# Attention steps of a decoder trunk: divisions on ScalarE, steps at mid-tile, a later begin with convolution taps held back

## The chip, the cores and the metric

The kernel runs on one core of a Trainium2 chip. The metric is the device time of one execution in microseconds. The engines are TensorE (PE, with its weight loads as PEld), VectorE (DVE), ScalarE (ACT), GpSimd (POOL) and SyncE (SP, which issues most transfers). Each engine works through its own queue of instructions in the order in which the program wrote them.

## The reference

One layer of a decoder trunk for a prompt of 2048 tokens and 8 x 4 sample tokens, D_MODEL 1024, in float32. The input projection gives queries (8 heads of 64), keys and values (2 heads), GLU halves for the convolution (512 channels) and two gates of 1024. The part that the change touches, cut down:

```python
def sink_softmax(s, mask, sink):
    s = jnp.where(mask, s, NEG_INF)
    m = jnp.maximum(jnp.max(s, axis=-1, keepdims=True), sink)
    p = jnp.exp(s - m)
    den = jnp.sum(p, axis=-1, keepdims=True) + jnp.exp(sink - m)
    return p / den

def swa_prompt(q, k, v, sinks):          # 16 blocks of 128 queries, each against 256 keys
    ...
    probs = sink_softmax(s, mask, sink)
    o = jnp.einsum('bnkgqs,bnskd->bnqkgd', probs.astype(v.dtype), vb)

def conv_branch(u_hist, conv_w, conv_b, ln_g, ln_b, w_conv_o):
    dw = causal depthwise convolution of width 31 over u = glu_a * sigmoid(glu_b), plus conv_b
    n = LayerNorm(dw)
    return jax.nn.silu(n) @ w_conv_o

# merge: (sigmoid(g_att) * (a @ w_attn_o) + sigmoid(g_conv) * conv) @ w_out, then residual and SwiGLU
```

Queries and keys are rotated on the first 16 of their 64 dims before the scores.

## The kernel before, in words

Everything is kept transposed, channels on the partitions. Tokens are worked on in two groups: group 0 has 1024 columns, in tiles of 512, group 1 has 1056 (the sample tokens last), in tiles of 352. Each float32 product is made of three reduced-precision ones, from operands split into a high and a low half (`hh`, `hl` for activations, `wh`, `wl` for weights). A weight's `wh` is written by ACT (`w_split`, line 242) and its `wl` by POOL (line 243), from raw weights that SP loads. A tile of the input projection is 24 matmuls; `in_order` gives the order of its columns: GLU pairs 0 and 1 (`gb`, `ga`), k, v, the four query tiles `q`, GLU pairs 2 and 3, and 16 gate tiles. `in_evac` empties each result: sigmoid of `gb` on ACT, the GLU product `u<-mm,sg` on DVE, copies of q, k, v and gates (`gst`) on ACT. Between the keys stand small adaLN products (`ada_unit`).

The program is written out in one fixed order by a planner in Python. `Timed` wraps DVE and TensorE: `V.t` and `T.t` add up the planned nanoseconds of what has been issued, by `dve_cost` and `pe_cost`. After each tile `pump` (line 458) lets other work in:

- one step of `tasks` (attention) if `T.t` has reached `task_t`, which then moves on by `task_dt`, 4200 here;
- the weight queue (`w_prefetch`): loads on SP, splits on ACT and POOL;
- one step of each generator in `soon` (the rotations, `rope`, line 953: transfers into `sw`, a product with the sine on POOL, then a product with the cosine and a sum on DVE, one for each pump);
- steps of `bg` for as long as `V.t < T.t + 1400`: mostly the 31 taps for each of four channel tiles of the convolution (`conv_gen`, line 1012; `dw<-u,cw,dw` on DVE, each planned at 1.2 us), then its LayerNorm and SiLU.

`in_done` (line 908) starts the rotation when a query tile is complete; for the fourth it also passes `then`, which appends `attn_gen` (line 1221) to `tasks` after the rotation's last sum and one more pump.

`attn_gen` first splits keys and queries of block 0 (`k_stack`, `q_stack`: high halves `kh`, `qst` on ACT, low halves `kl`, `qst` on POOL); in group 1 a step before it writes the key window out. Each of the group's 8 blocks then has four steps:

1. for the block before, transposes of its second head group and the product with the values (`o`, emptied by ACT as `oa`, `ob`); scores of the first four heads, row maxima on DVE (`p<-ps,mask`, `mx`), exponentials on ACT;
2. `attn_normalise` of these four: `den` and its reciprocal on DVE, four products on POOL (line 1195); the second product with values of the block before; scores of the other four heads;
3. `attn_normalise` of those; `v_block`: a transpose of the values into `pt` and its split into `vz`, high halves on ACT (line 1129), low halves on DVE;
4. transposes of the first four heads' probabilities and their split (`pth` on ACT, `ptl` on DVE); `k_stack` and `q_stack` of the next block.

After the last block `split` turns the four query tiles into `ah` (ACT) and `al` (DVE) for the output projection; group 1 attends the sample tokens before that. `mixer_out` (line 1410) begins by running whatever steps are still in `tasks`, with no tile between them.

PSUM has four buffers `mm` (tiles of the projection, `o`, half of the scores, the adaLN sum), two `ps` and two `pt`. `gemm` can already call `pump` after half of its matmuls (`mid`), which only the last tiles of the merge's output projection use.

Of the kernel before, what the change touches and what calls it, by code (L numbers as in the profile page):

```python
# [12 lines left out]
AF = mybir.ActivationFunctionType  # L13
ALU = mybir.AluOpType
# [115 lines left out]
class Builder:  # L130
# [379 lines left out]
    def gemm_group(self, keys, act, g, evac, hi_first=False, ready=None, chunks=None):  # L510

        units = [self.w_next(k) for k in keys]
        evs = [evac(k) for k in keys]
        chunks = chunks or GROUPS[g]["chunks"]
        for n, (c0, cw) in enumerate(chunks):
            while ready is not None and ready() < c0 + cw:
                self.step(self.bg)
            for u, ev in zip(units, evs):
                ps = self.gemm_tile(u, act, c0, cw, hi_first=hi_first)
                ev(ps, c0, cw)  # L520
                self.pump()
                if n == len(chunks) - 1:
                    self.w_done()
# [384 lines left out]
    def in_done(self, key):  # L908
        nc = self.nc
        kind, g, i = key  # L910
        W = GROUPS[g]["w"]
        if kind == "ga":
            self.u_ready[i] = True
            self.V.tensor_copy(self.uh[:, i], self.u[i][:, 1024:1024 + CW - 1])
            if i == 0:
                self.bg.append(self.conv_gen(g))
        elif kind == "k":
            self.rope(self.kg[:, 128:128 + W], self.sw[0], W)
        elif kind == "q":
            then = (lambda: self.tasks.append(self.attn_gen(g))) if i == 3 else None  # L920
            self.rope(self.q[i][:, :W], self.sw[(i + 1) % 2], W, then)
            if i == 3:
                self.cs = self.sw = None

    def mixer_in(self, g, skip=0):
        order = self.in_order(g)[skip:]
        if g == 1:
            self.boot_state()
            self.tasks += self.finals
            self.task_dt = 4000  # L930
            self.gemm_group(order[:3], self.h, g, self.in_evac, True, lambda: self.h_ready)
            for key in order[:3]:
                self.in_done(key)
            order = order[3:]
        for key in order:
            if key[0] == "k":
                while self.tasks:
                    self.step(self.tasks)
                self.gf = None
                self.task_dt = 4200  # L940
            self.gemm_group([key], self.h, g, self.in_evac)
            self.in_done(key)
            if key == ("gate", g, 14):
                self.gate_start(g)
            self.ada_next()
        self.h = None
# [6 lines left out]
    def rope(self, x, sw, W, then=None):  # L953
        nc = self.nc
        cos, sin = self.cs
        for b in (0, 64):
            nc.scalar.dma_start(out=sw[b:b + 8, :W], in_=x[b + 8:b + 16])
            nc.scalar.dma_start(out=sw[b + 8:b + 16, :W], in_=x[b:b + 8])
        nc.gpsimd.tensor_tensor(out=sw[:80, :W], in0=sw[:80, :W], in1=sin[:80, :W], op=ALU.mult)

        def rest():
            yield None
            self.V.tensor_tensor(out=x[:80], in0=x[:80], in1=cos[:80, :W], op=ALU.mult)
            yield None
            self.V.tensor_tensor(out=x[:80], in0=x[:80], in1=sw[:80, :W], op=ALU.add)
            if then is not None:
                yield None
                then()
        self.soon.append(rest())

# [218 lines left out]
    def attn_normalise(self, st):  # L1189
        nc = self.nc  # L1190
        P, den, es = st
        self.V.tensor_tensor(out=den, in0=den, in1=es, op=ALU.add)
        self.V.reciprocal(out=den, in_=den)
        for j in range(4):
            nc.gpsimd.tensor_scalar(out=P[j], in0=P[j], scalar1=den[:, j:j + 1], scalar2=0.0, op0=ALU.mult, op1=ALU.add)

    def attn_transpose(self, st):
        nc = self.nc
# [973 lines left out]
```

## Time and profile before

| what | value |
|---|---|
| median of 3 runs | 2930.61 us (2924.27 to 2932.72) |
| profiled execution, its own time | 2930.97 us |
| its span | 2927.8 us |
| mean granted TensorE clock | 0.973 |
| busy: PE, PEld, DVE, ACT, POOL | 2738.3, 2573.8, 2039.0, 1187.1, 1672.8 us |

The profile is one execution, with times in us from the start of the span. Input projection and attention of group 0 lie at about 190 to 535 us, those of group 1 at about 1280 to 1718 us. In the rows of a timeline stand start, duration, engine, line, operation, out<-in, shapes and the number of instructions merged, and in brackets the idle time before it on that engine and what ended it. Line 98 is the planner's wrapper, through which all matmuls and most DVE instructions go. In the rows of waits stand who waited for whom, the total, the number of times and the longest. In the rows by stretch PEclk is the TensorE clock that was granted, as a share of full speed.

### The profile page before, as it was taken

How to read it: one execution, taken by the hardware profiler on the slowest of the kernel's cores; microseconds unless marked ns; L12 is line 12 of the kernel's file. 1: busy time of each engine (PE TensorE's matmuls, PEld its weight loads, DVE VectorE, ACT ScalarE, POOL GpSimd, SP SyncE). 2: the span in 40 equal slices, each digit the busy share in tenths (PEclk: the TensorE clock that was granted, in tenths of full speed). 3: DMA queues.
4: the chain of work that ended last, by engine and by line, in shares of the span. 5: the costliest groups of instructions: out<-in, count | busy, mean ns of one | idle time of the engine just before them, and what ended most of it. 6: DMA issues, size and time to landing. Idle time of an engine off the chain costs nothing. (4 is left out here: it accounts for less than half of the span.)

```text
span 2927.8 us, 43739 instructions
## 1 busy us (share of the span) xinstructions
PE 2738.3 (94%) x16046; PEld 2573.8 (88%) x16046; DVE 2039.0 (70%) x3304; ACT 1187.1 (41%) x2410; POOL 1672.8 (57%) x1305
## 2 busy tenths in 40 slices
PE   8997899999899999998788999989999998999998
PEld 4775677789899999898778999979999997999997
DVE  5999963365766666779997436587766665677676
ACT  4334466433433333431555443343343334333333
POOL 1367776334666666455675222476677667666664
PEclk9998999999999999999899999999999998999999
DMA  7542232443222222431111333433333355222221
GB/s 279 151 115 69 76 104 91 139 141 124 89 76 75 85 80 73 127 103 44 40 57 60 102 120 125 152 122 100 112 114 105 102 187 167 66 76 76 80 72 63
DMA packets 364601, 302.94 MB, mean 103 GB/s; under 512 B 33483, under 2 KB 321111, under 8 KB 364365
## 3 DMA queue, kind: packets, MB, share of 16 engines
q1 hardware_dynamic: 347621, 276.02, 30.8%
q10 hardware_dynamic: 16768, 24.15, 2.6%
q8 instruction: 127, 2.08, 0.3%
q14 instruction: 85, 0.70, 0.1%
HBM read 249.98 MB, written 50.23 MB: 103 GB/s over the span
## 5 line engine op out<-in xcount | busy, mean ns | idle before, releaser
L243 POOL TENSOR_TENSOR wl<-wr,wh 128x512 fp32r<-128x512 f32 (+1 forms) x470 | 893.5, 1915 | 634.5 <-ACT wh L242 571.1
L98 PE MATMUL mm<-third,wh 128*128 128x352 f32 (+1 forms) x2323 | 568.4, 325 | 6.6 <-DVE u L98 3.7
L242 ACT ACTIVATE wh<-wr 128x512 fp32r<-128x512 f32 (+1 forms) x470 | 372.4, 810 | 282.2 <-PE mm L98 125.9
L98 PE MATMUL mm<-hh,wh 128*128 128x352 f32 (+1 forms) x1200 | 436.0, 363 | 30.5 <-DVE u L98 11.2
L98 PE MATMUL mm<-hh,wl 128*128 128x352 f32 (+1 forms) x1200 | 426.4, 355 | 0.0
L98 PEld LDWEIGHTS mm<-third,wh 128*128 128x128 f32 x2323 | 407.7, 190 | 12.1 <-DVE third L98 6.6
L98 PE MATMUL mm<-hl,wh 128*128 128x352 f32 (+1 forms) x1200 | 416.6, 356 | 1.3 <-DVE hl L98 1.3
L243 POOL TENSOR_TENSOR wl<-s,wh 128x512 fp32r<-128x512 f32 x198 | 259.1, 1317 | 261.8 <-ACT wh L242 249.7
L98 DVE SCALAR_TENSOR_TENSOR dw<-u,cw,dw 128x1024 f32<-128x1024 f32 x240 | 393.4, 1652 | 4.7
L98 PE MATMUL mm<-third,wl 128*128 128x352 f32 (+1 forms) x1187 | 383.2, 323 | 0.6 <-POOL wl L243 0.6
L98 PE MATMUL mm<-mh,wh 128*128 128x352 f32 (+1 forms) x1048 | 340.1, 325 | 3.4 <-DVE third L98 1.8
L98 PE MATMUL mm<-ml,wh 128*128 128x352 f32 (+1 forms) x1048 | 334.8, 324 | 4.2 <-ACT wh L242 2.5
L98 PE MATMUL pt<-third,wh 128*128 128x352 f32 (+1 forms) x1189 | 292.2, 325 | 10.9 <-ACT y L1982 5.3
L98 DVE SCALAR_TENSOR_TENSOR third<-mm,mod_G,third 128x352 f32<-128x352 f32 (+2 forms) x408 | 223.7, 565 | 95.5 <-PE mm L98 78.3
L98 PEld LDWEIGHTS mm<-hh,wh 128*128 128x128 f32 x1200 | 230.1, 192 | 63.2 <-DVE u L98 12.1
L242 ACT ACTIVATE wh<-s 128x512 fp32r<-128x512 f32 x198 | 120.9, 626 | 383.7 <-PE mm L98 190.7
L98 PE MATMUL mm<-mh,wl 128*128 128x336 f32 (+1 forms) x824 | 266.1, 323 | 5.7 <-POOL wl L243 5.7
L98 PEld LDWEIGHTS mm<-hl,wh 128*128 128x128 f32 x1200 | 228.8, 192 | 22.9 <-DVE hl L98 1.9
L98 PEld LDWEIGHTS mm<-hh,wl 128*128 128x128 f32 x1200 | 229.3, 191 | 21.5
L98 PEld LDWEIGHTS mm<-third,wl 128*128 128x128 f32 x1187 | 225.3, 190 | 0.9 <-POOL wl L243 0.9
L98 PEld LDWEIGHTS pt<-third,wh 128*128 128x128 f32 x1189 | 209.8, 191 | 12.7 <-ACT y L1982 5.8
L98 PEld LDWEIGHTS mm<-mh,wh 128*128 128x128 f32 x1048 | 200.3, 191 | 4.6 <-DVE third L98 2.1
(357 smaller groups left out, 5504.5 us busy)
## 6 DMA issues: line engine op xcount, KB each, us to landing
wr<-in_w_ffn_in SPq DMA_DIRECT2D x132, 512.0 KB
wr<-in_w_ffn_out SPq DMA_DIRECT2D x66, 512.0 KB
wr<-in_w_in SPq DMA_DIRECT2D x52, 512.0 KB
wr<-in_w_ada SPq DMA_DIRECT2D x48, 512.0 KB
wr<-in_w_out SPq DMA_DIRECT2D x32, 512.0 KB
gl<-gate SPq DMA_DIRECT2D x64, 176.0 KB
third<-op_p SPq DMA_DIRECT2D x56, 176.0 KB
gate<-gst ACTq DMA_DIRECT2D x48, 176.0 KB
```

What stands on the lines that cost most here:

```text
L98: return f(*args, **kw)
L242: self.nc.scalar.activation(out=hi, in_=src, func=AF.Copy)
L243: self.nc.gpsimd.tensor_tensor(out=lo, in0=src, in1=hi.bitcast(F32), op=ALU.subtract)
```

## The change

Four edits. The mid-tile `pump` is switched on in `gemm_group` for tiles of 512 columns while `tasks` is not empty, and `task_dt` is 6000 instead of 4200 in group 0. When the fourth query tile is done, the planner's DVE clock is put 10 us ahead, so that `pump` issues no `bg` work until TensorE's planned time has caught up; this holds in both groups. The rotation of the fourth query tile is followed by two pumps instead of one before `attn_gen` is appended. In `attn_normalise` the four products with the reciprocal are ACT activations (Copy with a scale for each partition) instead of POOL operations.

```diff
-                ps = self.gemm_tile(u, act, c0, cw, hi_first=hi_first)
+                ps = self.gemm_tile(u, act, c0, cw, hi_first=hi_first, mid=cw == 512 and len(self.tasks) > 0)
...
             then = (lambda: self.tasks.append(self.attn_gen(g))) if i == 3 else None
+            if i == 3:
+                self.V.t = max(self.V.t, self.T.t) + 10000
             self.rope(self.q[i][:, :W], self.sw[(i + 1) % 2], W, then)
...
-                self.task_dt = 4200
+                self.task_dt = 4200 if g else 6000
...
             if then is not None:
-                yield None
+                for _ in range(2):
+                    yield None
                 then()
...
         for j in range(4):
-            nc.gpsimd.tensor_scalar(out=P[j], in0=P[j], scalar1=den[:, j:j + 1], scalar2=0.0, op0=ALU.mult, op1=ALU.add)
+            nc.scalar.activation(out=P[j], in_=P[j], func=AF.Copy, scale=den[:, j:j + 1])
```

## The prediction

> **What bounds the kernel now.** I read the page first, then the busy time by stretch around the two attention stages, then TensorE's waits there, then the timelines of the engines that it waits for.
>
> ```profile
> span 2927.8 us, 43739 instructions
> PE 2738.3 (94%) x16046; PEld 2573.8 (88%) x16046; DVE 2039.0 (70%) x3304; ACT 1187.1 (41%) x2410; POOL 1672.8 (57%) x1305
> ```
> TensorE carries the span. A change elsewhere pays only where TensorE stands still or runs at a lowered clock.
> ```profile
> core 0: us, PE busy (x) PEld busy (x) DVE busy (x) ACT busy (x) POOL busy (x), PEclk, DMA share, GB/s
> 190.00:270.00 80.00, 62.08 (x253) 47.96 (x252) 78.55 (x80) 22.99 (x52) 56.73 (x32) 0.87 0.22 63
> 270.00:390.00 120.00, 104.94 (x479) 82.12 (x477) 114.27 (x155) 61.45 (x163) 94.81 (x85) 0.94 0.30 92
> 390.00:520.00 130.00, 127.03 (x610) 100.31 (x609) 51.85 (x160) 80.31 (x193) 76.68 (x102) 1.00 0.31 96
> 520.00:550.00 30.00, 23.70 (x98) 18.19 (x98) 13.51 (x14) 19.77 (x29) 12.36 (x8) 0.83 0.51 153
> 1380.00:1400.00 20.00, 5.63 (x25) 4.36 (x25) 19.79 (x19) 4.21 (x9) 18.01 (x13) 0.70 0.10 27
> 1400.00:1420.00 20.00, 14.82 (x75) 14.48 (x76) 17.64 (x41) 9.77 (x26) 5.09 (x9) 0.71 0.11 30
> 1440.00:1550.00 110.00, 96.34 (x577) 90.20 (x576) 103.59 (x177) 63.47 (x193) 82.88 (x94) 0.97 0.20 62
> 1550.00:1720.00 170.00, 159.92 (x994) 151.59 (x994) 84.11 (x216) 79.17 (x174) 61.31 (x82) 0.99 0.28 88
> ```
> Take width minus PE busy times PEclk as what a stretch loses: 26.0, 21.4, 3.0 and 10.3 us in group 0, 16.1, 9.5, 16.6 and 11.7 us in group 1, 115 us in all. Where DVE is busy 94 to 99% (the convolution taps) the loss is large; once the taps are over (390 to 520) it is 3 us, with the same attention blocks. So the loss is DVE's lateness, not the number of attention steps.
> ```profile
> PE ps L98 <- POOL qst L1162: 13.0, 5, 6.3
> PE mm L98 <- DVE u L98: 10.8, 2, 9.3
> PE mm L98 <- DVE mx L98: 5.2, 3, 4.4
> PE ps L98 <- POOL qst L1162: 13.3, 7, 5.0
> PE mm L98 <- DVE u L98: 8.0, 3, 5.1
> PE mm L98 <- DVE uh L98: 5.2, 1, 5.2
> PE pt L98 <- DVE vz L98: 4.8, 4, 1.8
> ```
> (TensorE's waits; three rows of 190 to 540 us, four of 1370 to 1640 us.) The deep single ones, and DVE's queue ahead of the first:
> ```profile
> 230.48 0.79 PE L98 MATMUL mm<-hh,wh 128*128 128x512 f32 x1 [9.25 <-DVE u L98]
> 318.34 0.61 PE L98 MATMUL ps<-kh,qst 128*128 128x288 f32 x1 [6.32 <-POOL qst L1162]
> 355.87 0.61 PE L98 MATMUL ps<-kh,qst 128*128 128x288 f32 x1 [4.36 <-POOL qst L1162]
> 544.78 0.65 PE L98 MATMUL mm<-al,wh 128*128 128x336 f32 x1 [2.10 <-DVE al L1387]
> 1387.88 0.61 PE L98 MATMUL ps<-kh,qst 128*128 128x288 f32 x1 [5.01 <-POOL qst L1162]
> ...
> 195.17 3.07 DVE L98 TENSOR_TENSOR q<-q,sw 80x1024 f32<-80x1024 f32 x1
> ...
> 203.13 7.96 DVE L98 SCALAR_TENSOR_TENSOR dw<-u,cw,dw 128x1024 f32<-128x1024 f32 x3
> ...
> 220.22 3.38 DVE L98 TENSOR_TENSOR q<-q,cosT 80x1024 f32<-80x1024 f32 x1
> ```
> The rotations stand in DVE's queue behind taps of up to 2.65 us each (7.96/3), which the planner costs at 1.2 us.
>
> **The change part by part.** The sum is made against the profiled execution: 2930.97 us, 3.2 outside its span of 2927.8, and 0.4 above the median shown, 2930.61.
>
> *Taps held back.* The planner's DVE clock jumps by 10 us when the last query group is done, in both groups. So no taps are issued for about 10 us of TensorE's work, some eight at 1.2 us, and the last two rotations and the GLU products run as soon as DVE has worked off what it holds. The taps are not saved: they come later, into stretches that are 94% full, and DVE's total stays. Ends: 0 (all handed back) and the 26.0 us of the first stretch, 25.6 of 1380 to 1420. What is left for good is the work TensorE does while no taps are queued: I take the 10 us in each group, -20. The convolution has room: the taps' end is followed by 130 us at 40% DVE in group 0.
>
> *Attention begun one pump later.* Every instruction of the first step moves: ACT's kh and qst, POOL's kl and qst, in group 1 a transpose, a copy and the key window's store; the mask load on SP moves with its own step, behind weight loads that stay. In group 0 the pump is followed by a mid-tile one, so the start slips half a tile. In group 1 the whole chain, the state loads on SP too, slips one tile and so does its end. The last split there:
> ```profile
> L1387 DVE TENSOR_TENSOR al<-q,ah x8: 1219/1254/3384, 535.8 to 1714.0; 128x1024 fp32r<-128x1024 f32 x4, 128x1056 fp32r<-128x1056 f32 x4
> ```
> It starts at 1714.0; a tile later it touches the output projection. Ends 0 and +4; I take +1.
>
> *Steps in the middle of 512-column tiles, 6000 apart.* Only group 0's input projection has such tiles. Before, one step a tile, by the planner's costs: 5182 ns of tile, some 430 of adaLN and 1385 of attention make 7.0 us a step. Now the 6000 decides. The 37 steps take 216 planned us from the middle of a tile on, of about 247 left, so the two query splits come four tiles before the gates end. Before, the last split came in the output stage: 10.3 us lost in 520 to 550 (the al wait above is part). Ends -10.3 and 0; I take -9, since the splits then lie beside gate tiles that wait for nothing of theirs. The weight queue is also served at mid-tile: SP's loads and the ACT and POOL halves of the splits come up to half a tile earlier; worth nothing, as no row of TensorE's waits in these stretches names a weight. If that cover went, one wl (3 us) would show.
>
> *Divisions from POOL to ACT.* 128 instructions leave POOL and come to ACT. The stretch that ends in the wait at 318.34:
> ```profile
> 302.32 0.18 DVE L98 RECIPROCAL den<-den 128x4 f32<-128x4 f32 x1
> 302.42 0.19 DVE L98 TENSOR_TENSOR vz<-pt,vz 128x64 fp32r<-128x64 f32 x1
> ...
> 303.04 5.54 DVE L98 SCALAR_TENSOR_TENSOR dw<-u,cw,dw 128x1024 f32<-128x1024 f32 x4
> ...
> 302.66 4.85 POOL L1195 TENSOR_SCALAR p<-p,den 128x256 f32<-128x256 f32 x4 [3.92 <-issue]
> 307.48 6.62 POOL L243 TENSOR_TENSOR wl<-wr,wh 128x1024 fp32r<-128x1024 f32 x2
> 314.06 2.83 POOL L1153 TENSOR_TENSOR kl<-kg,kh 64x128 fp32r<-64x128 f32 x2
> ...
> 302.64 0.22 ACT L1129 ACTIVATE vz<-pt 128x64 fp32r<-128x64 f32 x1 [3.78 <-DVE vz L98]
> 302.76 2.00 ACT L242 ACTIVATE wh<-wr 128x1024 fp32r<-128x1024 f32 x2
> ...
> 1437.54 1.86 POOL L1195 TENSOR_SCALAR p<-p,den 128x256 f32<-128x256 f32 x4 [5.92 <-ACT ob L1219]
> ...
> 1408.23 0.49 ACT L1185 ACTIVATE p<-p,mx 128x256 f32<-128x256 f32 x1
> ...
> 1436.30 0.59 ACT L1219 ACTIVATE oa<-mm 64x512 f32<-64x512 f32 x1
> ```
> Four divisions cost POOL 4.85 us beside taps and 1.86 alone. On ACT the nearest row is the exponential of the same shape, 0.49; without its accumulator read I take 0.4, four 1.6 us (ends 0.9, from half-height copies, and 2.0). The Copy behind exponentials at 1436.30 comes without a table load. The Trainium skill (ScalarE: Activation LUTs, What ACT_TABLE_LOAD costs) would price one at 492 ns, back-to-back ones overlapping by 93; no division on ACT is in this trace, and by it four are an estimated 1.7 us.
>
> POOL's gain: the wl no longer waits for four divisions, but its other half wh on ACT now waits 1.6 us behind them. Here POOL starts wl at about 306, not 307.5: 2 us off such a wait with what kl gains. Four waits of this kind; ends 0 and -26.3 (13.0+13.3); I take -6.
>
> ACT's price, vz: in the third step of a block the value split comes behind the divisions on ACT, and DVE's half of it behind that. DVE goes from reciprocal to vz at once (302.32, 302.42); now it stands about 1.95 us (1.6, a 0.22 copy, latency) before its next tap. 16 blocks, of which some nine lie where DVE is full: ends 0 and +17.6. I take +12, since DVE is short there but TensorE's waits give some of it cover.
>
> ACT's price, oa and ob: in the second step the divisions come ahead of the evacuation of o, and TensorE's next tile wants that buffer; it waits now already:
> ```profile
> 289.77 0.50 PE L98 MATMUL mm<-hh,wh 128*128 128x512 f32 x1 [0.35 <-ACT ob L1219]
> ```
> Ends 0 and 16 x 1.6 = +26; I take +4, nearer to the row.
>
> *Clock.* It falls to 0.70 to 0.94 around deep waits; (1 - PEclk) x PE busy is 8.1, 6.3, 1.7 and 4.3 us in four of the rows above, 20 in all. Without the 9 and 5 us waits about a third goes: -7 (ends 0, -20).
>
> Sum: -20 + 1 - 9 - 6 + 12 + 4 - 7 = -25, so **2906 us**.
>
> **The rivals.**
> *Taps only moved.* All held-back DVE work is handed back in the 94 to 99% stretches, and only the tail in group 0 is gained. For: DVE's total is unchanged. Against: DVE has 130 us at 40% behind the taps. -9 and -2 of clock: 2920 us.
> *ACT hands DVE's lateness on (slower).* ACT works in order; ACT's vz already waits 3.78 us for DVE at 302.64. With a division that waits for den ahead of oa/ob, every second step's next tile inherits that wait. It decides once den is later than about 1 us after TensorE's scores, the margin behind the 0.35 row. In nine blocks 3.78 + 1.6 us: +48, less the 25 with the ob term (4) already in it: 2930.97 - 29 + 48 = 2950 us. For: ACT busy only 51% in 270 to 390 yet with such waits. Against: DVE is less late after the hold.
> *DVE gets faster.*
> ```profile
> 1414.99 2.60 DVE L98 SCALAR_TENSOR_TENSOR dw<-u,cw,dw 128x1024 f32<-128x1024 f32 x2
> ```
> If taps were slowed by POOL's divisions as these are by taps, each four would give DVE 4.85 - 1.86 = 3 us; nine blocks of two fours, 54 us, of which the DVE-full stretches can use at most the 38 lost in 270 to 390 and 1440 to 1550; half of it brings 2887 us. Against: the four taps beside them took 1.39 us each (5.54/4), and taps with POOL idle 1.30 (2.60/2). The Trainium skill (GPSIMD Engine Reference, Specifications) says that POOL shares its SBUF interfaces with VectorE and contends with DVE instructions that have two SBUF inputs, as taps do; the trace agrees that they contend, but POOL pays nearly all of it.
>
> **How the numbers follow.** Forecast 0.45 (2891 to 2921), taps only moved 0.22 (2914 to 2926), ACT hands it on 0.18 (2925 to 2965), DVE faster 0.15 (2878 to 2891). About 0.3%, 9 us, is what a measurement here can tell. Faster: 0.45 + half of 0.22 + 0.15 = 0.71; same: the other half and 0.05 of the slower rival, 0.16; slower 0.13. The range 2879 to 2938 leaves out most of the slower rival and the lower tail.
>
> **What would show it.** The hold: the 9.25 and 5.01 waits gone, 1380 to 1400 above 12 us of PE busy. The tail: the last group-0 split well before the last gate tile, no al wait there. Divisions: POOL without L1195, wl earlier; DVE waiting about 2 us on ACT's vz in each block; waits on ob near the row. It is wrong if 270 to 390 or 1440 to 1550 loses more than before by over 10 us, or the ob waits sum to over 15 us.

## The result and the profile after

The changed kernel takes 2958.76 us (median of 4 runs, 2952.95 to 2963.21) against 2930.32 us for the kernel before (median of 4 runs). The ratio is 1.0102, with a 95% interval of 1.0088 to 1.0115: it is slower by 28 us, where 2906 us, 24 us faster, was forecast. The profiled execution of the changed kernel is the fastest of its four, 2952.95 us, 22 us above the profiled one before (2930.97).

The first lines of the page of the changed kernel (the same columns as before):

```profile
span 2951.2 us, 43674 instructions
PE 2756.8 (93%) x16046; PEld 2591.5 (88%) x16046; DVE 2016.7 (68%) x3304; ACT 1238.1 (42%) x2536; POOL 1617.2 (55%) x1177
```

The work went where the diff sends it: POOL's 128 divisions left (1305 to 1177 instructions, 56 us less), ACT has 126 more rows and 51 us more. Nothing of that says why TensorE ends later. The stretches help, though the same work lies up to 29 us later in the changed kernel, so that equal times no longer hold equal work. Changed kernel, with the columns shown in the prediction; the last row is the 30 us around the first matmul of group 0's output projection, 16 before it and 14 behind, which before the change were nearly the stretch 520 to 550:

```profile
190.00:270.00 80.00, 61.26 (x234) 47.25 (x233) 65.72 (x71) 25.01 (x58) 54.50 (x23) 0.83 0.22 63
270.00:390.00 120.00, 98.95 (x445) 77.01 (x444) 107.69 (x155) 69.59 (x184) 82.09 (x64) 0.91 0.25 79
390.00:520.00 130.00, 112.76 (x522) 88.15 (x521) 59.76 (x166) 91.48 (x222) 55.20 (x62) 0.95 0.23 73
520.00:550.00 30.00, 30.00 (x131) 23.67 (x130) 8.08 (x5) 11.16 (x14) 13.89 (x9) 1.00 0.47 145
1380.00:1400.00 20.00, 20.00 (x126) 20.00 (x125) 19.75 (x14) 2.12 (x4) 6.12 (x2) 1.00 0.21 53
1440.00:1550.00 110.00, 97.44 (x575) 92.15 (x573) 98.04 (x185) 77.49 (x225) 60.66 (x62) 0.95 0.18 57
1550.00:1720.00 170.00, 155.03 (x919) 145.93 (x920) 100.62 (x247) 93.64 (x229) 59.22 (x66) 0.96 0.25 78
548.60:578.60 30.00, 26.44 (x133) 22.27 (x133) 7.20 (x11) 14.43 (x20) 9.52 (x4) 0.97 0.56 175
```

By the prediction's measure (width minus PE busy times PEclk), group 0 now loses 29.2, 30.0 and 22.9 us in the first three stretches where it lost 26.0, 21.4 and 3.0. So 8.6 us more is lost in 270 to 390, and 19.9 us more in 390 to 520, where DVE is busy only 46% of the time. That stretch was the prediction's proof that attention steps cost nothing once the taps are over. The first matmul of group 0's output projection slips from 535.8 to 564.6 us (+28.8). The stretch 520 to 550, which loses 0.0 us, is therefore no longer the tail: around that matmul 4.4 us are lost where 10.3 were, so about half of the tail went. In the same way 1380 to 1400 loses nothing only because group 1's attention now begins later; in the kernel with mid-tile steps alone, without the hold, that stretch is as full (19.84 us of PE busy). Group 1's first such matmul slips from 1717.7 to 1744.9 (+27.2), so in the profile the loss stands complete at the end of group 0. That group 1 adds none is a balance: with the divisions alone the two slips are 9.2 and 21.3 us, and with the other three edits alone 25.4 and 14.7.

Who waits for whom in the changed kernel, TensorE, 190 to 540 us (total, times, longest):

```profile
PE mm L98 <- DVE u L98: 11.1, 3, 4.6
PE pt L98 <- DVE ptl L98: 8.7, 5, 4.0
PE mm L98 <- DVE mx L98: 8.5, 5, 2.8
PE mm L98 <- issue: 6.4, 3, 2.4
PE ps L98 <- DVE csum L98: 5.6, 1, 5.6
PE ps L98 <- DVE mx L98: 5.2, 1, 5.2
PE ps L98 <- POOL qst L1165: 3.4, 2, 1.9
```

The wait for `qst` fell from 13.0 to 3.4 us, more than forecast. The single wait of 9.25 us for `u` is now 4.61, but the waits for `u` sum to 11.1 us as before (10.8). Beside them stand many waits of 2 to 5 us on whatever the attention step needs next; the one for `csum`, 5.6 us, is the convolution's LayerNorm, which now comes after 390. The wait of 5.2 us for `mx` has a plain cause: DVE wrote `mx` late, since it waited for the mask. DVE's timeline in the changed kernel, then SP's transfers:

```profile
251.20 0.42 DVE L98 CUSTOM_DVE_ANT_0 p<-ps,mask 128x256 f32<-128x256 f32 x1 [10.10 <-DMA mask<-const_mask]
```
```profile
244.71 0.37 SPq L347 DMA_DIRECT2D wr<-in_w_in  x1
247.04 0.37 SPq L381 DMA_DIRECT2D wr<-in_w_ada  x1
247.50 0.42 SPq L1256 DMA_DIRECT2D mask<-const_mask  x1
```

The first block's mask is loaded by SP behind two weight loads, the first of which stood 25.3 us until POOL's `wl` was done with its buffer. It is issued at 247.50 (before the change at 227.45, first row below), and DVE, the fullest engine there, stands still for 10.1 us in the stretch where it has least room. SP's row before, and its longest wait in the changed kernel:

```profile
227.45 0.45 SPq L1253 DMA_DIRECT2D mask<-const_mask  x1
```
```profile
SPq L347 <- POOL wl L243: 25.3, 1, 25.3
```

### The profile page after: what moved, and what is told of

Same layout as the page of the kernel before. It is cut to its first block, busy times and chain, and to the rows that moved or that the text cites. A ratio compares the mean times of both kernels' runs of the same rounds, so it can differ in the third digit from the quotient of the medians.

```text
span 2951.2 us, 43674 instructions
## 1 busy us (share of the span) xinstructions
PE 2756.8 (93%) x16046; PEld 2591.5 (88%) x16046; DVE 2016.7 (68%) x3304; ACT 1238.1 (42%) x2536; POOL 1617.2 (55%) x1177
## 5 line engine op out<-in xcount | busy, mean ns | idle before, releaser
L98 PE MATMUL mm<-hh,wh 128*128 128x352 f32 (+1 forms) x1200 | 444.5, 371 | 25.9 <-DVE u L98 14.2
L98 PE MATMUL mm<-hh,wl 128*128 128x352 f32 (+1 forms) x1200 | 433.1, 361 | 0.0
L98 DVE SCALAR_TENSOR_TENSOR dw<-u,cw,dw 128x1024 f32<-128x1024 f32 x240 | 375.3, 1585 | 3.6
L98 PEld LDWEIGHTS mm<-hh,wl 128*128 128x128 f32 x1200 | 234.1, 195 | 22.1
```

Of the source, the lines that this page charges most:

```text
L98: return f(*args, **kw)
```

## The experiments

Each kernel ran beside the kernel before on one chip; the medians of the kernel before were 2930.05, 2929.79, 2930.11, 2928.74 and 2930.32 us in the five sets, and differences are taken within a set.

### The parts, each alone

```diff
divisions alone
-            nc.gpsimd.tensor_scalar(out=P[j], in0=P[j], scalar1=den[:, j:j + 1], ...)
+            nc.scalar.activation(out=P[j], in_=P[j], func=AF.Copy, scale=den[:, j:j + 1])
mid-tile steps alone
+ mid=cw == 512 and len(self.tasks) > 0
+ self.task_dt = 4200 if g else 6000
hold alone
+            if i == 3:
+                self.V.t = max(self.V.t, self.T.t) + 10000
the change with the divisions back on POOL: all but the first of these, and the later begin
```

Divisions alone. 

> The kernel before, with the divisions on ACT alone. Theory D (ACT, working in order, hands DVE's lateness on: vz, oa and ob behind the divisions) expects most of the loss here, +20 to +35 us, with DVE waiting about 40 us for ACT's vz as in the changed kernel (42.6). Theory M (the mid-tile steps are the loss: a tile in progress keeps a fifth mm buffer, and the weight queue served at mid-tile gets ahead of the mask load on SP) expects -5 to +10.

Mid-tile steps alone. 

> The kernel before, with the mid-tile steps and the 6000 alone. Theory M expects +15 to +35 us: waits on o or score buffers in front of the fourth score of a step, 390 to 520 us losing over 10 us where the kernel before loses 3. Theory D expects -10 (the splits of the queries ahead of the gates' end) to +5.

Hold alone. 

> The kernel before, with the taps held back alone. The prediction's term is -20 us (10 in each group) with the waits of 9.25 us at 230 and 5.0 at 1388 gone. The rival, taps only moved, expects 0 to -5 us.

The change with POOL's divisions. 

> The changed kernel with the divisions back on POOL. Theory D expects the loss to go: 2915 to 2930 us. Theory M expects it to stay within 12 us of the changed kernel's 2959.

Measured: divisions alone 2947.04 us (+17.0; ratio 1.0067, 1.0052 to 1.0082), mid-tile steps alone 2950.82 (+20.8; 1.0075, 1.0058 to 1.0092), hold alone 2924.45 (-5.6; 0.9981, 0.9972 to 0.9991), the change with POOL's divisions 2946.62 (+16.6; 1.0065, 1.0050 to 1.0080). Neither of the two theories is the whole: the divisions and the mid-tile steps each cost, about equally, and the hold brings a quarter of what it was given.

The hold alone, its stretches where something changed:

```profile
190.00:270.00 80.00, 65.47 (x276) 50.78 (x275) 76.07 (x82) 28.88 (x70) 57.79 (x35) 0.89 0.27 82
390.00:520.00 130.00, 124.74 (x592) 98.59 (x591) 52.92 (x152) 79.23 (x186) 75.12 (x96) 0.97 0.31 98
```

190 to 270 loses 21.7 instead of 26.0 us, but 390 to 520 loses 9.0 instead of 3.0: what the hold gains early in group 0 is handed back later. TensorE's waits show what it does, and what it doesn't:

```profile
228.92 0.61 PE L98 MATMUL ps<-kh,qst 128*128 128x288 f32 x1 [3.98 <-POOL qst L1164]
235.37 0.61 PE L98 MATMUL mm<-kh,qst 128*128 128x288 f32 x1 [5.12 <-POOL qst L1164]
1389.08 0.61 PE L98 MATMUL ps<-kh,qst 128*128 128x288 f32 x1 [5.63 <-POOL qst L1164]
```

In group 0 the 9.25 us on `u` are gone, and 9.1 us on `qst` stand in their place. In group 1 the wait for `qst` stays (5.63, before 5.01); gone are the waits behind it, on `u` and `uh` (5.12, 2.46 and 5.18 us before), and a wait of 5.6 us on `vst` is new. Group 0's output projection begins 2.6 us earlier than before (533.2), group 1's 4.5 us earlier (1713.2).

### The later begin, and the mask's load

```diff
later begin alone
+                for _ in range(2):
+                    yield None
mask's load a step earlier (in attn_gen, group 0, ahead of the first yield 0)
+        if g == 0:
+            mask0 = self.tmp("mask0", 256)
+            nc.sync.dma_start(out=mask0, in_=self.a["mask"][1])
...
-                nc.sync.dma_start(out=mask, in_=self.a["mask"][1])
```

All four edits with the earlier load. 

> All four edits, with the load of the first block's mask issued one attention step earlier, ahead of the weight loads that it stood behind. Theory SP order (the mask's load behind two weight loads is what made DVE stand 10.1 us at 251): that stand goes, 190 to 270 loses some 8 us less than its 29.2, the time falls from 2959 to about 2949 to 2953. Rival, ACT and the buffers set the pace anyway (the taps that DVE missed there are only pushed about): 2956 to 2960, the output projection of group 0 starting at 562 to 565 as before this edit.

Later begin alone. 

> The kernel before with the attention begun one pump later and nothing else. The prediction's term was +1 with ends 0 and +4; by the sum of the others (the three measured alone give 17 + 21 - 6 = 32 against 28 for all) it is -4 to +4: 2926 to 2934. A start behind weight loads on SP, as with all four edits, would show as a stand of DVE on the mask of over 5 us.

Later begin with the earlier load. 

> The kernel before with the attention begun one pump later, and the first mask's load a step earlier. Theory mask (the later step's load stands on SP behind two weight loads that wait for free raw buffers, DVE stands 10.2 us on it): 2928 to 2933. Rival, the later begin itself (the attention ends a tile later and its splits reach the output projection): 2936 to 2940.

Measured: the whole change with the earlier load 2947.85 us, 11 us below the 2958.76 of the change without it (18.1 above its own set's before, against 28.4). The later begin alone costs 9.6 us (2939.75; 1.0031, 1.0019 to 1.0043), and with the earlier load 3.3 us (2932.05; 1.0010, 1.0002 to 1.0019). I had put the late mask down to the mid-tile pump; the later begin alone has it too. DVE and SP in that kernel:

```profile
259.80 0.42 DVE L98 CUSTOM_DVE_ANT_0 p<-ps,mask 128x256 f32<-128x256 f32 x1 [10.21 <-DMA mask<-const_mask]
```
```profile
226.23 0.37 SPq L381 DMA_DIRECT2D wr<-in_w_ada  x1
253.13 0.37 SPq L347 DMA_DIRECT2D wr<-in_w_in  x1
255.47 0.37 SPq L381 DMA_DIRECT2D wr<-in_w_ada  x1
255.94 0.42 SPq L1254 DMA_DIRECT2D mask<-const_mask  x1
```

SP issues nothing for 27 us, then two weight loads, then the mask. In the kernel before the mask goes out at 227.45, right behind such a load; in the kernel with mid-tile steps alone at 225.8, and DVE doesn't wait for it. So the load's place costs 6.3 us alone and 10.4 in the whole change.

### What the divisions cost on ACT

```diff
value split first (third step)
-            self.attn_normalise(cur["s1"])
             self.v_block(g, n, (bi + 1) % 3)
+            self.attn_normalise(cur["s1"])
and product with the values first (second step)
-            self.attn_normalise(s0)
             if prev:
                 pv_second()
+            self.attn_normalise(s0)
```

Divisions on ACT, value split first. 

> The kernel before with the divisions on ScalarE alone, but in the third step of a block the value split is written ahead of the divisions, so that ACT does vz's high halves first. Theory vz (the divisions cost by DVE's stand of some 1.9 us per block on ACT's vz): most of the 17 us goes, 2930 to 2937, and DVE's waits on vz fall to what they were. Rival, the buffer of o (oa and ob behind the divisions in the second step): the time stays at 2944 to 2948. Both in equal parts: about 2938 to 2941.

Both orders changed. 

> As the last, and in the second step the product with the values and oa, ob are also written ahead of the divisions. Theory that order on ACT is all that the divisions cost: 2920 to 2931, the kernel before less what POOL gained (up to 6 us). Rival, the divisions cost because they themselves come later on ACT than on POOL and the transposes of the probabilities wait for them: no better than 2940. With the vz theory alone true this run equals the last one within 3 us.

Measured: 2937.96 us with the value split first (1.0029, 1.0018 to 1.0040), 2932.23 with both (1.0011, 1.0002 to 1.0020). Of the 17.0 us, about 9 go with the order in the third step (`vz` behind the divisions), about 6 with that in the second (`oa` and `ob` behind them), and about 2 are left. TensorE's waits fit that. Divisions alone: one row of 190 to 540 us, one of 1370 to 1640 us.

```profile
PE mm L98 <- DVE mx L98: 18.9, 6, 6.2
PE pt L98 <- DVE vz L98: 8.3, 6, 3.1
```

With the value split first the second row is no longer among the largest there, and the first stays at 17.3 us. With both orders changed it reads:

```profile
PE mm L98 <- DVE mx L98: 5.3, 3, 4.4
```

which is what it was before (5.2). What the swaps show is the price of the order, not that one wait alone makes it: each also moves `den` and its reciprocal on DVE, and the value split first takes DVE's waits for ACT's `vz`, in both attention stages (190 to 540 and 1370 to 1720), only from 48.0 to 35.7 us (before 15.3). ACT's timeline in the changed kernel shows the order that both edits undo: the divisions wait 5.43 us for `den`, that is for DVE, and `vz`, which needs nothing of `den`, stands behind them.

```profile
290.50 1.69 ACT L1198 ACTIVATE p<-p,den 128x256 f32<-128x256 f32 x4
292.20 0.59 ACT L1222 ACTIVATE oa<-mm 64x512 f32<-64x512 f32 x1
...
303.13 1.71 ACT L1198 ACTIVATE p<-p,den 128x256 f32<-128x256 f32 x4 [5.43 <-DVE den L98]
304.74 0.20 ACT L1132 ACTIVATE vz<-pt 128x64 fp32r<-128x64 f32 x1
```

### What the mid-tile steps cost

```diff
o in pt:            o = self.pt() if kv else self.mm()
attention's step alone at mid-tile (in gemm):
+                elif self.T.t >= self.task_t:
+                    self.task_t = max(self.task_t, self.T.t - 3000) + self.task_dt
+                    self.step(self.tasks)
7000 apart:         self.task_dt = 4200 if g else 7000
```

Mid-tile steps alone, second product in a `pt` buffer. 

> The kernel before with the mid-tile steps alone, and the second product with the values put into a pt buffer instead of an mm one, so that a second step takes two mm buffers instead of three. Theory buffers (a step in the middle of a tile needs the mm buffer that was filled just ahead of the tile in progress, half a tile earlier than at a tile's end; the fourth scores stand 18 us in all in the kernel with mid-tile steps alone): the stands of the second steps go, 2951 falls to 2936 to 2943, and the output projection of group 0 starts at 543 to 549 instead of 557. Rival, the weight queue and taps let in at mid-tile (work on SP, ACT, POOL and DVE ahead of the attention's): 2947 to 2952.

Mid-tile steps alone, only the attention's step let in. 

> The kernel before with the mid-tile steps alone, but at the middle of a tile only the attention's step is let in: the weight queue, the rotations, the taps and the convolution's LayerNorm wait for the tile's end as before. Theory pump as a delay (generators that hand back None count pumps, so with twice the pumps the wait that was a tile between a producer and its reader becomes half a tile: csum 0.7, dg 3.7 and 1.6, and taps and weight splits go ahead of attention's work): most of the 20 us goes, 2922 to 2936, without waits on csum and dg. Rival, the steps themselves (an attention step every tile and some in the middle make the chain of scores, maxima and exponentials tighter than DVE, POOL and ACT can follow): 2944 to 2952, with the stands of the scores on mx, p and qst left as they are.

The last with the hold. 

> The last one with the taps held back as well. If the two edits add up, it lies 4 to 7 us below the last one; if that is below 2924 it beats the kernel before and the hold alone. If the steps in the middle are themselves the cost, 2938 to 2946.

Both covers away. 

> The kernel before with the mid-tile steps alone, at mid-tile the attention's step alone, and the second product with the values in a pt buffer. Theory two covers (the short mm buffers and the pumps that count as delays each hid behind the other): with both away 2928 to 2938, no stands on csum or dg and under 8 us on the mm scores. Rival, the denser steps themselves meet a late DVE (taps are still running until about 390): 2943 to 2951, with the stands moved to transposes and first scores.

Both away, 7000 apart. 

> As mid_pt_only (2946), with steps 7000 planned ns apart in group 0 instead of 6000: about the pace of one step a tile, at places in the tile's middle and end. Theory pace (denser steps meet a late DVE and a full POOL): the cost goes, 2928 to 2936. Rival, the place in the tile (the step cuts a tile in two, and what TensorE reads next is asked for half a tile earlier): 2940 to 2947.

Both away, divisions on ACT in the better order. 

> As mid_pt_only (2946), with the divisions on ACT behind the value split and behind oa, ob; alone these divisions gave 2932. Theory POOL (mid-tile steps cost because four divisions of up to 4.85 us stand ahead of qst, kl and wl on POOL more often): 2928 to 2936, with POOL's waits gone. Rival, DVE and the pace: 2942 to 2950, as before this edit.

Measured: 2949.88, 2947.78, 2940.77, 2945.98, 2941.24 and 2948.91 us, ratios 1.0066, 1.0066, 1.0031, 1.0059, 1.0039 and 1.0063, each within 0.0015. Four of my theories fall here: the short buffers, the pumps that count as delays, the two together, and POOL's divisions. The group of the scores that use an `mm` buffer (busy us, mean ns, idle us before them, 190 to 540 us), in the kernel before, for the mid-tile steps alone, with `o` in `pt`, and with the attention's step alone, one fence each:

```profile
L98 PE MATMUL mm<-kh,qst 128*128 128x288 f32 x32 | 10.2, 331 | 0.0
```
```profile
L98 PE MATMUL mm<-kh,qst 128*128 128x288 f32 x32 | 11.6, 367 | 18.0 <-POOL p L1195 5.2 <-POOL qst L1162 4.9 <-issue 3.8
```
```profile
L98 PE MATMUL mm<-kh,qst 128*128 128x288 f32 x32 | 10.0, 324 | 5.4 <-POOL qst L1162 3.2 <-issue 2.1
```
```profile
L98 PE MATMUL mm<-kh,qst 128*128 128x288 f32 x32 | 11.6, 366 | 21.0 <-issue 7.5 <-ACT gst L908 6.6 <-POOL wl L243 5.5
```

A step in the middle of a tile asks for an `mm` buffer that was filled just ahead of the tile in progress, and taking one buffer off the step takes 12.6 us of these stands away, as expected; yet the time falls by 0.7 us, and TensorE then stands elsewhere (8.2 us on `csum`, 0.7 without that edit; 13.2 on `u`, 10.8 without). Letting only the attention's step in at mid-tile leaves no `csum` wait, but the scores' stands (21.0). Nor are these stands the price by themselves: all mended, below, has 22.1 us of them and is no slower than the kernel before. The hold brings 7.0 us in this company (17.7 to 10.7 above before), about what it brings alone. With both away 2946 us is left. The divisions on POOL are not it either (2948.91). The pace is a part: steps 7000 apart instead of 6000 bring 6 us (17.2 to 10.9 above before). The stretches of 6000, then of 7000, both with both covers away (the last row of each is again the 30 us around group 0's first matmul of the output projection):

```profile
270.00:390.00 120.00, 100.27 (x447) 80.13 (x447) 106.15 (x164) 58.12 (x156) 86.19 (x87) 0.89 0.24 75
390.00:520.00 130.00, 117.14 (x548) 92.18 (x549) 60.70 (x157) 80.22 (x186) 75.85 (x98) 0.96 0.27 86
539.80:569.80 30.00, 26.44 (x130) 22.27 (x130) 7.20 (x11) 14.39 (x20) 9.52 (x4) 0.96 0.57 177
```
```profile
270.00:390.00 120.00, 102.74 (x467) 80.97 (x466) 111.38 (x155) 59.39 (x159) 91.89 (x84) 0.93 0.29 88
390.00:520.00 130.00, 120.65 (x559) 94.33 (x558) 50.39 (x158) 77.39 (x188) 72.09 (x100) 0.95 0.27 85
532.90:562.90 30.00, 26.70 (x125) 21.74 (x124) 15.29 (x15) 17.48 (x22) 12.37 (x8) 0.94 0.47 144
```

Losses 30.8 and 17.5 us at 6000, 24.5 and 15.4 at 7000, against 21.4 and 3.0 before: at the slower pace the full stretch is nearer to before. The tail loses 4.6 and 4.9 us where it lost 10.3, so it gains about half of that in both. At 7000, 190 to 270 loses 29.9 us, 4 more than before. What is left of the price, some 12 us in 390 to 520, has no single place: there it is seven waits of 0.4 to 2.9 us on `mx`, `gst`, `ob` and others, 9.35 in all, and 6.0 of lowered clock. It is neither the buffer nor the pumps nor POOL's divisions alone. That it is the place in the tile, half a tile less between a step and what reads it, is argued and not shown.

### The change with its causes mended

```diff
all mended: the four edits + mask's load earlier + both orders on ACT + attention's step alone at mid-tile
all mended, o in pt: the same + o = self.pt() if kv else self.mm()
mended without mid-tile steps: hold + later begin + mask's load earlier + divisions with both orders
```

All mended. 

> All four edits, with the four things mended that the runs so far point to: the first mask's load a step earlier, the value split ahead of the divisions, the product with the values ahead of the divisions, and at the middle of a tile the attention's step alone. If the prices add up (mask 11, order on ACT 15, pumps 15 to 20): 2915 to 2925 from 2959. If they overlap, since each wait taken away uncovers another: 2928 to 2938.

All mended, `o` in `pt`. 

> All four edits with the four mends and the second product in a pt buffer. Its mm scores stood 22.1 us without that; if these go and nothing takes their place: 2910 to 2918. If they are replaced: 2922 to 2930.

Mended without mid-tile steps. 

> The change without the mid-tile steps: taps held back, later begin with the first mask's load a step earlier, divisions on ACT behind the value split and behind oa and ob. If the steps in the middle cost their 15 to 20 us in company too: 2908 to 2918, faster than both kernels. If the mends that made room for them were what counted: 2922 to 2930.

Measured: 2927.71 us (0.9994, 0.9984 to 1.0003), 2925.53 (0.9984, 0.9975 to 0.9994) and 2924.34 (0.9981, 0.9972 to 0.9990). The mends, with the hold's own gain of 5.6 us among it, take back the whole loss of 28 us: all mended can't be told from the kernel before, and with `o` in `pt` it is 3.2 us faster. So together they cover what made the change slow, though not one by one: they overlap, and the better expectations (2910 to 2918 with `o` in `pt`, 2908 to 2918 without mid-tile steps) are missed. Mended without mid-tile steps, and hold alone with 2924.45, are the fastest kernels here, 0.2% below the kernel before. In this company the mid-tile steps cost only 1 to 2 us: without them the tail loses its 10 us again (rows below, mended without mid-tile steps, whose output projection begins at 540.1), with them the middle loses more.

```profile
270.00:390.00 120.00, 108.85 (x503) 84.47 (x502) 113.09 (x166) 73.92 (x190) 74.76 (x65) 0.97 0.27 86
520.00:550.00 30.00, 22.71 (x99) 17.29 (x98) 13.99 (x13) 20.68 (x30) 12.08 (x8) 0.85 0.51 156
```

Lost here: 14.4 and 10.7 us. All mended with mid-tile steps loses 29.1 in the same middle and 4.1 around its first matmul of the output projection (544.8). Why the steps cost 11 to 21 us in the kernels above and 2 here stays open; none of those has the hold, the later begin, the mask's load in time and the divisions in the better order all together.

## Why the prediction was wrong, by its steps

*What bounds the kernel.* "So the loss is DVE's lateness, not the number of attention steps" failed. It was read from 390 to 520 with one step a tile. With denser steps and DVE just as idle (55.50 us busy), the same stretch loses 15.0 us in the kernel with mid-tile steps alone:

```profile
390.00:520.00 130.00, 119.84 (x555) 92.89 (x554) 55.50 (x142) 78.87 (x182) 69.13 (x90) 0.96 0.27 86
```

The stretch showed that one step a tile was covered, and I took it to show that steps are free. The signs that the prediction set for being wrong were set elsewhere and stayed silent: 270 to 390 lost 8.6 us more, 1440 to 1550 0.9 more, both under 10, and no wait for `ob` is among TensorE's larger ones.

*Mid-tile steps, forecast -9.* Alone +20.8. About half of the gain that was priced came (around the first matmul of the output projection 5.4 us are lost instead of 10.3, with no `al` wait); the cost had no term at all, and its ends, -10.3 and 0, excluded any. This is the step that failed most, by 30 us. The scores' buffer, the pumps that count as delays and the pace had no term. The kernel before shows 0.0 idle ahead of the scores in `mm`, and I took what did not wait for free. What the runs show in its place is a cost of 20.8 us, of which a slower pace takes off 6; where the rest comes from stays open.

*Taps held back, forecast -20, and clock, -7.* Alone -5.6, clock included. The mechanism is right in part: the waits for `u` and `uh` go, but in group 0 as much waiting on `qst` takes their place, and group 1's 5.01 us on `qst`, which the hold was to remove, stays. The size is wrong: the first rival, "taps only moved", is nearer to what happened to this term. Its sign, 1380 to 1400 above 12 us of PE busy, tells little, since without the hold a later group 1 fills that stretch too. The clock did not recover: (1 - PEclk) x PE busy in group 0's first three stretches is 10.4, 8.9 and 5.6 us after, where 8.1, 6.3 and 0 was lost before, although the deepest wait there is now 5.6 us instead of 9.25.

*Later begin, forecast +1.* Alone +9.6, of which 6.3 goes with the mask's load. The sentence "the mask load on SP moves with its own step, behind weight loads that stay" named the event, and no price was put on it; the rows of SP's queue around it, which would have shown loads held up by full buffers, were not read. That is where this term failed.

*Divisions, forecast +10 (12 + 4 - 6).* Alone +17.0. `vz` cost 9 and `oa`, `ob` 6, close to the 12 and 4, each by the order that removes it. POOL's gain failed: with both orders changed 2 us of cost are left and no gain. The wait on `qst` did shrink in group 0 (13.0 to 6.6 us), but not in group 1 (13.3 to 15.5). POOL itself then waited for the half of the weight split that stays on ACT. POOL's idle time ahead of `wl`, 190 to 540 us, before and with both orders changed:

```profile
L243 POOL TENSOR_TENSOR wl<-wr,wh 128x1024 fp32r<-128x1024 f32 x42 | 116.0, 2781 | 75.9 <-ACT wh L242 38.4 <-issue 37.5
```
```profile
L243 POOL TENSOR_TENSOR wl<-wr,wh 128x1024 fp32r<-128x1024 f32 x43 | 117.8, 2759 | 143.1 <-ACT wh L242 104.9 <-issue 33.4 <-PE mm L98 4.9
```

Before, 38.4 us of that idle time ended with ACT's `wh`, now 104.9: the engine relieved waits for the engine loaded. That this ate POOL's gain is argued, not shown; TensorE's own wait for `wl` there is 0.7 us.

*The rivals.* "ACT hands DVE's lateness on", at 2950 us and with a chance of 0.18, has the measured 2958.76 in its range (2925 to 2965), and the divisions do wait for `den` on ACT ahead of `oa` and `ob` (5.74 us at 292.89 with the divisions alone). Yet its number is luck: it gave that order 48 us, where swapping it brought about 6, and it kept the -9 of the mid-tile steps, which cost 20.8 alone. The four parts measured alone sum to 41.8 us; the whole costs 28.4, so they don't add up. "DVE gets faster" came at a third of its size and without its gain: DVE's busy time fell by 18 us with the divisions alone (2039.0 to 2021.1) and by 22 with all four edits (to 2016.7), where the rival had 54, and TensorE ended no earlier.

## What to carry to other kernels

When a step is moved by one slot, list every queue that it issues to and read that queue's rows there: a 0.4 us transfer put behind two stalled loads cost 6 to 10 us here. When work is moved to another engine, write first what a third engine waits for, and only then the moved work (here 15 of 17 us came back by two swapped calls). That a profile shows no wait holds for the present spacing of the steps only; a denser spacing needs a term of its own whose upper end is not zero. And when two profiles drift apart, compare stretches that hold the same work, not the same times: read at 520 to 550 the tail seems gone, read around its first matmul half of it is left.

## What the runs showed of the hardware

Four ACT copies with a scale of 128x256 took 1.69 and 1.71 us, one 494 ns in the median:

```profile
L1198 ACT ACTIVATE p<-p,den x128: 491/494/512, 256.7 to 1631.2; 128x256 f32<-128x256 f32 x128
```

I had taken 0.4 and 1.6 us from the exponential of that shape. By the formula of the Trainium skill (ScalarE: Activation LUTs, What ACT_TABLE_LOAD costs) one takes an estimated 492 ns, and two in a row overlap by about 93. The trace agrees: (4 x 494 - 1700) / 3 is 92 ns. The exponentials alone, 0.49 us each in the prediction's row, would have said the same, had I not taken off an accumulator read that the timeline lists as a row of its own (kernel before):

```profile
1408.14 0.18 ACT L1185 ACTIVATION_READ_ACCUMULATOR p<-p,mx 128x1 f32 x1
```
